# A decoder layer on one core: the first h chunk by hand within the first weight piece, and a few steps later in the order

## The chip, the core and the metric

The kernel runs on one core of a Trainium2 chip. Five engines work side by side, each through its own queue in program order: TensorE (PE, matrix products; PEld is its weight load), VectorE (DVE), ScalarE (ACT), GpSimd (POOL) and SyncE (SP), which here issues nearly all DMAs. The metric is the device time of one execution in microseconds, as the median of several runs. A profile is one further execution, recorded instruction by instruction.

## The reference, cut to what matters

One layer of a hybrid decoder, 256 tokens of width 2048, in float32:

```python
shift, scale, gate = jnp.split(jax.nn.silu(c) @ w_ada + b_ada, 3, axis=-1)
h = rms_norm(x, norm_pre_w) * (1.0 + scale[:, None]) + shift[:, None]
proj = h @ w_in
...
y_a = o_a.reshape(b, s, GDN_V_WIDTH).astype(x.dtype) @ w_proj_gdn
...
h_b = jax.nn.sigmoid(ml_o) * h_b * jax.nn.silu(ml_z)
y_b = h_b.astype(x.dtype) @ w_proj_mlstm
merged = jax.nn.sigmoid(gate_a) * y_a + jax.nn.sigmoid(gate_b) * y_b
out = merged @ w_out
return x + gate[:, None] * rms_norm(out, norm_post_w)
```

Between proj and y_a stands a gated delta rule (GDN), between proj and y_b an mLSTM, both in chunks. What matters here: no product with w_in can begin before h is there, and h needs the statistics of x and, for each of 16 chunks of 128 channels, a shift and a scale, which are sums over a row of w_ada.

## The kernel before, in words

**Products.** Every product of weights is made of three in float32r: operands are split into a high part (a cast on ScalarE, L169) and a low part (a subtraction on VectorE or POOL, L170), and mm3 (L223) adds hi x hi, hi x lo and lo x hi into one PSUM tile. split_w (L174 on) decides by a running share which low parts POOL makes; VectorE makes the others.

**The stream.** Weights come as units of up to one megabyte through three buffers (load_w, tile raw). A unit is used in pieces of 1024 columns. Stream.run fixes the order by hand: it prepares pieces (casts and low parts) as long as no more than `ahead` of them are pending, then issues the products of one piece, then calls side.step(). The work beside the products, attention and gates, stands in generators; each gets one turn per step, and `yield` means one step later. Each engine runs what it is given in the order of issue. Units of w_ada (tile ar, three buffers) stand in the same stream without products: VectorE multiplies one with silu(c) along the row and sums it (L353). w_ada units 2k and 2k + 1 give the shift and the scale of chunk k.

**The start groups.** Fourteen groups of 512 columns of w_in are accumulated in seven blocks over the chunks of h (BLOCKS), so that products can begin when chunk 0 alone is known: the first block takes groups 0 to 5 over chunk 0, two groups to a unit, the second groups 6 to 13 over chunks 0 and 1, and so on. Sums between the blocks are kept in SBUF (part): a copy on ScalarE in the first two blocks (L411, some on VectorE, L413), an addition on VectorE later (L409). In the last block the finished group gets Sigmoid or Silu at once (L418), and is stored to DRAM (L420) or multiplied with its neighbour and stored (L422, L423).

**The start itself.** SyncE issues c, the two halves of c_row, x, an identity, two small tables, and then the stream's loads. c_row gets Silu and is spread over all partitions by eight TensorE instructions on one row (L280). The sums of squares of x go to ScalarE and VectorE (L291, L292), the power to POOL. Then ScalarE scales x by its row statistics, two chunks at a time (x_scale, L300), TensorE turns them (x_turn, L306) and ScalarE copies them back (L308): chunks 0 to 7 are scaled, and 0 to 3 turned, ahead of the stream; the others behind the w_ada units. h_chunk (L327 to L331) makes shift, scale, hf, and its two parts h_hi and h_lo.

**Later places.** gates (L455 on) computes decay and gate rows beside the last block and ends in transposes (L507, L508). mlstm_out (L992) turns the finished mLSTM output, gated by gated_by (L1023). merge (L1181 to L1190) adds the two branches and turns the sum for the last product.

Of the kernel before, what the change touches and what calls it, by code (L numbers as in the profile page):

```python
# [117 lines left out]
def hybrid_layer_kernel(  # L118
# [50 lines left out]
        A.copy(hi, src)  # L169
        (eng or V).tensor_tensor(lo, src, hi.bitcast(F32), op=ALU.subtract)  # L170

    share = [-3072.0, START_SHARE]

    def split_w(src, hi, lo):  # L174

# [50 lines left out]
    bp = x0 = y0 = None  # L226


    ct = const("ct", c_t, [P, KC])
    sil = cp.tile([P, KC], F32, name="sil")  # L230
    A.activation(sil, ct, AF.Silu)
# [37 lines left out]
    crow = [part[4 + i].rearrange("p b c -> p (b c)")[0:1] for i in range(2)]  # L269
    for i in range(2):  # L270
        SP.dma_start(crow[i], c_row[:, i * 1024:(i + 1) * 1024])
    for b in range(2):
        SP.dma_start(xs[:, b], x[b * P:(b + 1) * P])
    SP.dma_start(ident, consts[:, 0:128])
    bat = const("bat", b_ada_t, [P, 32])
    npre = const("npre", npre_t, [P, KC])
    for i in range(2):
        A.activation(crow[i], crow[i], AF.Silu)
    for q in range(4):
        T.matmul(csil[:, q * 512:(q + 1) * 512], one_row, crow[q // 2][:, (q % 2) * 512:(q % 2 + 1) * 512],  # L280
                 start=True, stop=True)
    late_c = {}

    def late_consts():
        SP.dma_start(con[:, 128:512], consts[:, 128:512])
        late_c.update(gcv=const("gcv", gconv, [P, 256]), mcv=const("mcv", mconv, [P, 64]),
                      abb=const("abb", ab_bias, [P, 1]), alog=const("alog", a_log, [32, 1]),
                      gnw=const("gnw", gnorm, [P, 1]), mnw=const("mnw", mnorm_t, [P, KC]))

    for b in range(2):  # L290
        A.activation(part[2].rearrange("p b c -> p (b c)"), xs[:, b, 0:1024], AF.Square, accum_out=ss[:, b, 0:1])  # L291
        V.scalar_tensor_tensor(part[3].rearrange("p b c -> p (b c)"), xs[:, b, 1024:D], 1.0, xs[:, b, 1024:D],  # L292
                               op0=ALU.mult, op1=ALU.mult, accum_out=ss[:, b, 1:2])
    V.tensor_reduce(rs, ss, axis=AX.X, op=ALU.add)
    V.tensor_scalar(rs, rs, 1.0 / D, EPS, op0=ALU.mult, op1=ALU.add)
    pow_(rs, rs, mhalf[:, 0:2])

    def x_scale(k):
        for b in range(2):
            A.activation(xs[:, b, k * P:(k + 2) * P], xs[:, b, k * P:(k + 2) * P], AF.Copy, scale=rs[:, b:b + 1])  # L300

    def x_turn(k):
        ps = jtile("xps")
        for b in range(2):
            for kk in range(2):
                T.transpose(ps[:, (b * 2 + kk) * P:(b * 2 + kk + 1) * P], xs[:, b, (k + kk) * P:(k + kk + 1) * P],  # L306
                            ident)
        A.copy(xs[:, :, k * P:(k + 2) * P], ps.rearrange("p (b c) -> p b c", b=2))  # L308
# [9 lines left out]
    V.scalar_tensor_tensor(bnp, bat[:, KC:2 * KC], 1.0, npre, op0=ALU.add, op1=ALU.mult)  # L318

    def load_ada(src):  # L320
        raw = sp.tile([P, 2048], F32, name="ar", tag="ar", bufs=ADA_BUFS)
        SP.dma_start(raw, src)
        return raw

    def h_chunk(k):

        A.activation(sh[:, k:k + 1], ad[:, k:k + 1], AF.Identity, bias=bat[:, k:k + 1])  # L327
        A.activation(s1[:, k:k + 1], ad[:, KC + k:KC + k + 1], AF.Identity, bias=bnp[:, k:k + 1],
                     scale=npre[:, k:k + 1])
        hf = sp.tile([P, S], F32, name="hf", tag="hf", bufs=2)  # L330
        A.activation(hf.rearrange("p (b t) -> p b t", b=2), xs[:, :, k * P:(k + 1) * P], AF.Identity, bias=sh[:, k:k + 1], scale=s1[:, k:k + 1])  # L331
        split(hf, h_hi[:, k], h_lo[:, k], V if k < 2 else G)

    stream = Stream(load_w, side, 2)
    NG, NE = len(START), 6
# [11 lines left out]
    def ada_units():  # L347

        adders = []
        for k in range(KC):  # L350
            for pt in range(2):
                def prep(h, raw, k=k, pt=pt):
                    V.scalar_tensor_tensor(raw, raw, 1.0, csil, op0=ALU.mult, op1=ALU.mult,  # L353
                                           accum_out=ad[:, pt * KC + k:pt * KC + k + 1])
                    j = 2 * (2 * k + pt) - 4
                    if 4 <= j < 16:
                        x_turn(j)
                        if j < 12:
                            x_scale(j + 4)
                    h_chunks(k - 1)  # L360
                    if pt == 1:
                        due.append(k)
                        if k == 0:
                            h_chunks(0)
                        elif k == KC - 1:
# [27 lines left out]
    def add_start_groups(bi):  # L393
# [12 lines left out]
        def after(g, ps):  # L406
            for b in range(2):
                if k0:
                    V.tensor_tensor(part[g][:, b], ps[b], part[g][:, b], op=ALU.add)  # L409
                elif bi or g < 4 or b == 0:  # L410
                    A.copy(part[g][:, b], ps[b])  # L411
                else:
                    V.tensor_copy(part[g][:, b], ps[b])  # L413
            if bi == len(BLOCKS) - 2 and g == 3:
                late_consts()
            if lastb:
                pt = part[g].rearrange("p b c -> p (b c)")
                A.activation(pt, pt, AF.Silu if g in (9, 11, 13) else AF.Sigmoid)  # L418
                if g < 8:
                    SP.dma_start(gate_dr[g], part[g])  # L420
                elif g % 2:
                    V.tensor_tensor(part[g], part[g], part[g - 1], op=ALU.mult)  # L422
                    SP.dma_start(gate_dr[8 + (g - 8) // 2], part[g])  # L423
                if g == NG - 1:
                    branches_open()

        adders = []
# [22 lines left out]
    def gates(ps):  # L450
# [50 lines left out]
        A.activation(g2[64:72], bm[64:72], AF.Exp, scale=-1.0)  # L501
# [22 lines left out]
        stream.add(w_ab, prep_w, use, after=lambda: side.add(gates(st_["ps"])))  # L524

    ada = ada_units()
    ia = 0
    for bi, (groups, k0, nk, first, last) in enumerate(BLOCKS):
        if bi == len(BLOCKS) - 1:
            add_ab()  # L530
        fs = add_start_groups(bi)
        for j, f in enumerate(fs):
            ahead = first + (last - first) * j / len(fs)
            while ia < len(ada) and ia < ahead:
                ada[ia]()
                ia += 1
            f()

# [217 lines left out]
    def gdn_stage2(zg, res, zr):  # L756
# [116 lines left out]
        for g, z, h, c in heads:  # L873
# [127 lines left out]
    def mlstm(m):  # L1001
# [29 lines left out]
        def gated_by(sg, first):  # L1031
            while "hn" not in r or not (first or "gated" in r):
                yield
            for b in range(2):
                gate(b, sg[:, b], first)
            r["gated"] = True
            yield
            if not first:
                yield from mlstm_out(m, r)

        def gated():
# [128 lines left out]
    def merge(hf, yb):  # L1170
# [213 lines left out]
```

## Time and profile before

| | before |
|---|---|
| median of 3 runs | 1620.76 us (1618.08 to 1620.88) |
| the profiled execution | 1616.79 us |
| its span | 1615.0 us |
| TensorE, products, share of the span | 98% |
| VectorE, ScalarE, POOL | 71%, 58%, 15% |
| DMA | 372.37 MB, 231 GB/s in the mean |

A row of the order of time gives the start, the duration, engine, line, operation and tiles, how many instructions were merged into the row, and in brackets the idle time ahead with what ended it. A row of waits gives who waited, for whom, the microseconds in total, the times and the longest. Products overlap in the pipeline, so a product's duration is longer than the distance between the starts of two.

### The profile page before, as it was taken

The page shows a single profiled execution, that of the slowest core. Times are in us where ns is not written, and L with a number is a line of the kernel's source. Part 1 is how long each engine was busy: PE and PEld are TensorE (multiplying, and loading weights), DVE is VectorE, ACT ScalarE, POOL GpSimd, SP SyncE. Part 2 cuts the span into 40 slices and gives each one's busy share as a digit, 9 for nine tenths or more (in the row PEclk, how much of TensorE's full clock was granted, in tenths as well). Part 3 has the DMA queues.
Part 4 walks back from the last instruction along what each step waited for, and adds up shares of the span by engine and source line. Part 5 has one row for each costly group of instructions (what it writes and reads, how often), then busy time and mean ns, then how long its engine had stood idle before and what let it go on. Part 6 is the DMA issues. An engine that isn't in the chain of part 4 may idle for free.

```text
span 1615.0 us, 25449 instructions
## 1 busy us (share of the span) xinstructions
PE 1585.7 (98%) x9844; PEld 1388.1 (86%) x9844; DVE 1148.3 (71%) x1798; ACT 936.4 (58%) x1497; POOL 235.2 (15%) x191
## 2 busy tenths in 40 slices
PE   7999999899999999999999999999999999999998
PEld 4888888689999999999999999889988788888886
DVE  6685555675689878887888888776778556756654
ACT  7744445664666575757666666664665544444443
POOL 1787761000000000000000000000010000100100
PEclk9999999999999999999999999999999999999999
DMA  9898775665555546454646464557778668767573
GB/s 375 342 408 334 263 286 191 236 244 204 181 182 191 183 170 193 171 191 158 205 159 197 157 196 169 184 211 246 281 291 315 222 247 293 280 233 250 196 275 115
DMA packets 96261, 372.37 MB, mean 231 GB/s; under 512 B 26262, under 2 KB 46214, under 8 KB 58252
## 3 DMA queue, kind: packets, MB, share of 16 engines
q1 hardware_dynamic: 96140, 370.75, 64.5%
q8 instruction: 77, 1.26, 0.3%
q14 instruction: 44, 0.36, 0.1%
HBM read 354.40 MB, written 16.31 MB: 230 GB/s over the span
## 4 chain that ended last, share of the span: by engine, by line
PE 88%; DVE 3%; ACT 3%; issue 2%; DMA 2%; POOL 1%; SPq 0%; DVEq 0%; POOLq 0%; ACTq 0%
PE pn L223 31%; PE pt L223 29%; PE py L223 16%; PE pw L223 5%; ACT whi L169 2%; DVE wlo L170 1%; DMA raw<-in_dram 1%; DVE part L409 1%; PE psa L223 1%; DMA ar<-in_dram 1%; PE mz L808 1%; PE mq L799 1%; PE po L848 0%; PE pa L820 0%; PE pc L838 0%
## 5 line engine op out<-in xcount | busy, mean ns | idle before, releaser
L170 DVE TENSOR_TENSOR wlo<-raw,whi 128x1024 fp32r<-128x1024 f32 x454 | 560.6, 1245 | 266.6 <-ACT whi L169 265.4
L169 ACT CAST whi<-raw 128x1024 fp32r<-128x1024 f32 (+1 forms) x517 | 532.1, 1046 | 314.3 <-PE pn L223 148.8
L223 PE MATMUL pt<-h_hi,whi 128*128 128x256 f32 x1280 | 368.8, 288 | 0.0
L223 PE MATMUL pt<-h_hi,wlo 128*128 128x256 f32 x1280 | 363.0, 284 | 0.0
L223 PE MATMUL pt<-h_lo,whi 128*128 128x256 f32 x1280 | 362.8, 283 | 0.0
L223 PE MATMUL pn<-whi,h_hi 128*128 128x512 f32 x896 | 354.2, 395 | 7.9 <-ACT whi L169 5.8
L223 PE MATMUL pn<-wlo,h_hi 128*128 128x512 f32 x896 | 351.1, 392 | 3.3 <-DVE wlo L170 2.5
L223 PE MATMUL pn<-whi,h_lo 128*128 128x512 f32 x896 | 349.9, 390 | 0.0
L223 PEld LDWEIGHTS pt<-h_hi,whi 128*128 128x128 f32 x1280 | 246.0, 192 | 1.4
L223 PEld LDWEIGHTS pt<-h_lo,whi 128*128 128x128 f32 x1280 | 246.2, 192 | 0.3
L223 PEld LDWEIGHTS pt<-h_hi,wlo 128*128 128x128 f32 x1280 | 246.0, 192 | 0.0
L223 PEld LDWEIGHTS pn<-whi,h_hi 128*128 128x128 f32 x896 | 168.7, 188 | 45.7 <-ACT whi L169 6.2
L223 PEld LDWEIGHTS pn<-wlo,h_hi 128*128 128x128 f32 x896 | 168.7, 188 | 41.6 <-DVE wlo L170 7.4
L223 PEld LDWEIGHTS pn<-whi,h_lo 128*128 128x128 f32 x896 | 168.5, 188 | 35.3
L170 POOL TENSOR_TENSOR wlo<-raw,whi 128x1024 fp32r<-128x1024 f32 (+1 forms) x63 | 146.1, 2327 | 67.2 <-ACT whi L169 65.0
L223 PE MATMUL py<-whi,yhi 128*128 128x512 f32 x384 | 150.6, 392 | 0.0
L223 PE MATMUL py<-whi,ylo 128*128 128x512 f32 x384 | 149.6, 390 | 0.0
L223 PE MATMUL py<-wlo,yhi 128*128 128x512 f32 x384 | 149.5, 389 | 0.0
L409 DVE TENSOR_TENSOR part<-pn,part 128x512 f32<-128x512 f32 x112 | 73.5, 685 | 52.4 <-PE pn L223 52.4
L169 ACT CAST yhi<-ya 128x512 fp32r<-128x512 f32 x48 | 29.9, 622 | 131.7 <-PE py L223 129.0
L170 DVE TENSOR_TENSOR ylo<-ya,yhi 128x512 fp32r<-128x512 f32 x48 | 33.2, 691 | 91.3 <-ACT yhi L169 89.5
L585 DVE SCALAR_TENSOR_TENSOR qs<-pt,gcv,qs 128x255 f32<-128x255 f32 (+2 forms) x192 | 92.1, 480 | 4.6
(244 smaller groups left out, 1785.2 us busy)
## 6 DMA issues: line engine op xcount, KB each, us to landing
raw<-in_dram SPq DMA_DIRECT2D x259, 1024.0 KB
ar<-in_dram SPq DMA_DIRECT2D x32, 1024.0 KB
raw<-in_dram SPq DMA_DIRECT2D x16, 512.0 KB
ya<-o_dr SPq DMA_DIRECT2D x32, 256.0 KB
gate_dr<-part SPq DMA_DIRECT2D x11, 512.0 KB
gb<-rows SPq DMA_DIRECT2D x20, 256.0 KB
raw<-in_dram SPq DMA_DIRECT2D x6, 768.0 KB
ug<-ud SPq DMA_DIRECT2D x32, 128.0 KB
```

What stands on the lines that cost most here:

```text
L169: A.copy(hi, src)
L170: (eng or V).tensor_tensor(lo, src, hi.bitcast(F32), op=ALU.subtract)
L223: T.matmul(ps, l, r, start=start and i == 0, stop=stop and i == 2, skip_group_check=True)
L409: V.tensor_tensor(part[g][:, b], ps[b], part[g][:, b], op=ALU.add)
L585: V.scalar_tensor_tensor(dst[:, n, sh:], src[:, 0:S - sh], taps(n, 3 - sh), dst[:, n, sh:], op0=ALU.mult, op1=ALU.add)
L799: T.matmul(psp[64:128, m * 64:(m + 1) * 64], um(m)[0:64, 64:128], y0[:, m], start=True, stop=True)
L808: T.matmul(psz[0:64, m * 64:(m + 1) * 64], p2[64:128, m], x0[64:128, m, 64:128], start=True, stop=True)
```

## The change

1. The DMA of c and its Silu move from the start to late_consts, behind other late loads; the Silu is two steps behind.
2. c_row goes as one DMA into an ar buffer, issued by ScalarE's queue. w_ada unit 0 (the shift of chunk 0) is loaded ahead of x, unit 1 (its scale) in two halves behind x and the tables. The two no longer stand in the stream, which begins with a weight unit.
3. Chunk 0 is made by hand inside the preparation of the first weight piece (first_chunk): five products of zeros; sums of squares, three quarters on ScalarE; statistics on POOL; the sums of the two w_ada units on VectorE, the second by halves; the cast of the weights; scaling and turning of chunks 0 and 1; one more product of zeros; the low part of the weights; hf straight from PSUM, h_hi, h_lo; the copy of chunk 1.
4. Scaling of chunks 2 to 7 and the turn of 2 and 3 move from the start to behind groups 1, 3 and 5 of the first block.
5. The values of a finished group (Sigmoid or Silu, store) become a side generator of rank 0 that begins one step later; the product of two neighbours comes one further step later.
6. One step more: before the gates' transposes, before the transposes of the last GDN group (`2 + zg // 7`), before mlstm_out of the first mLSTM group, before the merge's transposes.
7. POOL's share of low parts starts from -2048 instead of -3072, as the first piece is no longer counted.

The core of the diff:

```diff
-    share = [-3072.0, START_SHARE]
+    share = [-2048.0, START_SHARE]
+    begin = []
...
+        if begin:
+            begin.pop()(raw[:, 0:n], hi, lo)
+            return hi, lo
...
+    crow = ada_tile()[0:1]
+    A.dma_start(crow, c_row)
+    ar0, ar1 = load_ada(w_ada[0]), ada_tile()
     for b in range(2):
         SP.dma_start(xs[:, b], x[b * P:(b + 1) * P])
...
+        SP.dma_start(ar1[:, i * 1024:(i + 1) * 1024], w_ada[1][:, i * 1024:(i + 1) * 1024])
...
+    def keep_busy(n):
+
+        for _ in range(n):
+            T.matmul(zps, zero[:, 0:P], zero, start=True, stop=True)
...
-    for k in range(0, 8, 2):
-        x_scale(k)
-        if k in (2, 4):
-            x_turn(k - 2)
...
+    def first_chunk(src, hi, lo):
+
+
+        keep_busy(5)
...
+        G.tensor_tensor(rs, ss[:, :, 0], ss[:, :, 1], op=ALU.add)
+        G.tensor_scalar(rs, rs, 1.0 / D, EPS, op0=ALU.mult, op1=ALU.add)
+        pow_(rs, rs, mhalf[:, 0:2])
+        ada_sum(ar0, slice(0, D), ad[:, 0:1])
+        V.scalar_tensor_tensor(bnp, bat[:, KC:2 * KC], 1.0, npre, op0=ALU.add, op1=ALU.mult)
+        for i in range(2):
+            ada_sum(ar1, half[i], adh[:, i:i + 1])
+        V.tensor_tensor(ad[:, KC:KC + 1], adh[:, 0:1], adh[:, 1:2], op=ALU.add)
+        V.scalar_tensor_tensor(s1[:, 0:1], ad[:, KC:KC + 1], npre[:, 0:1], bnp[:, 0:1], op0=ALU.mult, op1=ALU.add)
+        A.activation(sh[:, 0:1], ad[:, 0:1], AF.Identity, bias=bat[:, 0:1])
+        A.copy(hi, src)
+        x_scale(0)
+        xps = x_turn(0)
+        keep_busy(1)
+        V.tensor_tensor(lo, src, hi.bitcast(F32), op=ALU.subtract)
+        hf = sp.tile([P, S], F32, name="hf", tag="hf", bufs=2)
+        A.activation(hf.rearrange("p (b t) -> p b t", b=2), xps[:, :, 0], AF.Identity, bias=sh[:, 0:1],
+                     scale=s1[:, 0:1])
+        split(hf, h_hi[:, 0], h_lo[:, 0], V)
+        A.copy(xs[:, :, P:2 * P], xps[:, :, 1])
+    begin.append(first_chunk)
...
-                pt = part[g].rearrange("p b c -> p (b c)")
-                A.activation(pt, pt, AF.Silu if g in (9, 11, 13) else AF.Sigmoid)
...
+                side.add(gate_values(g), 0)
...
+        def gate_values(g):
+
+            yield
+            pt = part[g].rearrange("p b c -> p (b c)")
+            A.activation(pt, pt, AF.Silu if g in (9, 11, 13) else AF.Sigmoid)
...
+                    if bi == 0 and gg in (1, 3, 5):
+                        x_scale(gg + 1)
+                        if gg == 1:
+                            x_turn(2)
...
-        yield from wait(2)
+        yield from wait(3)
         tp = gtile("tp")
...
-        yield from wait(2)
+        yield from wait(2 + zg // 7)
         yield from free(4)
...
             if not first:
+                yield
                 yield from mlstm_out(m, r)
...
-        yield
+        yield from wait(2)
         for k2 in range(hf * 4, hf * 4 + 4):
```

More of the change, by code (lines that the diff above doesn't have):

```diff
@@ L268, in hybrid_layer_kernel, with ada_tile, load_ada @@
     csil = pcs.enter_context(tc.tile_pool(name="pcs", bufs=1, space=PSUM)).tile([P, D], F32, name="csil")
-    crow = [part[4 + i].rearrange("p b c -> p (b c)")[0:1] for i in range(2)]
-    for i in range(2):
-        SP.dma_start(crow[i], c_row[:, i * 1024:(i + 1) * 1024])
+    def ada_tile():
+        return sp.tile([P, 2048], F32, name="ar", tag="ar", bufs=ADA_BUFS)
+    def load_ada(src):
+        raw = ada_tile()
+        SP.dma_start(raw, src)
+        return raw
+    crow = ada_tile()[0:1]
+    A.dma_start(crow, c_row)
+    ar0, ar1 = load_ada(w_ada[0]), ada_tile()
     for b in range(2):
@@ new lines, in x_turn, with ada_sum @@
+        return ps.rearrange("p (b k t) -> p b k t", b=2, k=2)
+    bnp = sp.tile([P, KC], F32, name="bnp")
+    adh = sp.tile([P, 2], F32, name="adh")
+    def ada_sum(raw, cols, out):
+        V.scalar_tensor_tensor(raw[:, cols], raw[:, cols], 1.0, csil[:, cols], op0=ALU.mult, op1=ALU.mult,
+                               accum_out=out)
+    def first_chunk(src, hi, lo):
+        keep_busy(5)
+        half = [slice(i * 1024, (i + 1) * 1024) for i in range(2)]
+        for b in range(2):
+            for i in range(2):
+                if b == 0 and i == 1:
+                    V.scalar_tensor_tensor(part[3].rearrange("p b c -> p (b c)"), xs[:, b, half[i]], 1.0,
+                                           xs[:, b, half[i]], op0=ALU.mult, op1=ALU.mult, accum_out=ss[:, b, i:i + 1])
+                else:
+                    A.activation(part[2].rearrange("p b c -> p (b c)"), xs[:, b, half[i]], AF.Square,
+                                 accum_out=ss[:, b, i:i + 1])
+        G.tensor_tensor(rs, ss[:, :, 0], ss[:, :, 1], op=ALU.add)
[3 more added lines that the diff above has]
+        V.scalar_tensor_tensor(bnp, bat[:, KC:2 * KC], 1.0, npre, op0=ALU.add, op1=ALU.mult)
+        for i in range(2):
+            ada_sum(ar1, half[i], adh[:, i:i + 1])
[12 more added lines that the diff above has]
+        A.copy(xs[:, :, P:2 * P], xps[:, :, 1])
@@ L349, in ada_units @@
         adders = []
-        for k in range(KC):
+        for k in range(1, KC):
             for pt in range(2):
@@ L533, in hybrid_layer_kernel @@
             ahead = first + (last - first) * j / len(fs)
-            while ia < len(ada) and ia < ahead:
-                ada[ia]()
+            while ia - 2 < len(ada) and ia < ahead:
+                ada[ia - 2]()
                 ia += 1
@@ L1038, in gated_by @@
             if not first:
+                yield
                 yield from mlstm_out(m, r)
```

50 lines of the change are left out of this document (22 added, 28 removed).

## Prediction

> **What bounds the kernel now.** I read the page first, then the waits of TensorE, then each engine's order of time in the first 36 us, then the other places where TensorE waits.
>
> ```profile
> span 1615.0 us, 25449 instructions
> PE 1585.7 (98%) x9844; PEld 1388.1 (86%) x9844; DVE 1148.3 (71%) x1798; ACT 936.4 (58%) x1497; POOL 235.2 (15%) x191
> ```
>
> ```profile
> PE pn L223 <- ACT whi L169: 5.8, 1, 5.8
> PE csil L280 <- ACT part L278: 3.9, 1, 3.9
> PE pn L223 <- DVE wlo L170: 2.5, 6, 0.6
> PE mpt L992 <- DVE hn L1023: 1.8, 2, 1.5
> PE pn L223 <- DVE part L409: 1.6, 3, 0.7
> PE tp L508 <- ACT work L501: 1.1, 1, 1.1
> ```
>
> TensorE is busy 98% of the span. Its real products stay as they are, so a change can win only where TensorE stands or runs slowly: ahead of its first real product, in the last block of the start groups, at the mLSTM output, at the merge. For the first place, SyncE's first and fourth issue, then VectorE, ScalarE and TensorE:
>
> ```profile
> 0.74 0.39 SPq L157 DMA_DIRECT2D ct<-in_dram  x1
> ```
>
> ```profile
> 1.82 0.83 SPq L273 DMA_DIRECT2D xs<-in_dram  x2
> ```
>
> ```profile
> 15.14 2.29 DVE L353 SCALAR_TENSOR_TENSOR ar<-ar,csil 128x2048 f32<-128x2048 f32 x1
> ```
>
> ```profile
> 17.90 0.60 ACT L331 ACTIVATE hf<-xs,sh,s 128x256 f32<-128x256 f32 x1
> 18.53 0.40 ACT L169 CAST h_hi<-hf 128x256 fp32r<-128x256 f32 x1
> 18.84 1.99 ACT L169 CAST whi<-raw 128x1024 fp32r<-128x1024 f32 x2
> 21.68 1.04 ACT L169 CAST whi<-raw 128x1024 fp32r<-128x1024 f32 x1 [0.86 <-DMA raw<-in_dram]
> ```
>
> ```profile
> 3.92 7.19 PE L280 MATMUL csil<-part,one_row 1*128 1x512 f32 x8 [3.92 <-ACT part L278]
> 12.20 1.97 PE L306 MATMUL xps<-con,xs 128*128 128x128 f32 x8 [1.09 <-ACT xs L300]
> 19.93 0.79 PE L223 MATMUL pn<-whi,h_hi 128*128 128x512 f32 x1 [5.76 <-ACT whi L169]
> ```
>
> ```profile
> 24.80 0.39 PE L223 MATMUL pn<-whi,h_lo 128*128 128x512 f32 x1
> 25.03 0.40 PE L223 MATMUL pn<-whi,h_hi 128*128 128x512 f32 x1
> ```
>
> The second w_ada unit is summed from 15.14; hf, h_hi and the first weight cast then stand in a row on ScalarE, and the first real product starts at 19.93. The product at 25.03 is the thirteenth, the first of the second weight unit. One starts 0.23 us after another (24.80, 25.03), so twelve should take 2.7 us; they took 5.1. The stretches just behind decide most of my forecast:
>
> ```profile
> 24.00:34.00 10.00, 10.00 (x46) 7.78 (x45) 8.09 (x10) 8.97 (x17) 0.96 (x1) 1.00 1.01 403
> 34.00:49.00 15.00, 13.81 (x66) 10.68 (x65) 7.04 (x8) 14.94 (x28) 11.77 (x6) 1.00 1.02 418
> ```
>
> The columns behind the length are the busy times of TensorE, its weight loads, VectorE, ScalarE and POOL, then clock, DMA share and GB/s. ScalarE has 8.97 of 10 us and then 14.94 of 15; TensorE loses 1.2 us in the second. In the ramp ScalarE is the bound.
>
> **The start.** SyncE no longer issues c and c_row ahead of x; the shift unit goes first, so the first megabyte is issued at 0.74 instead of 1.82. The DMA share is 1.01 and 1.02, so all that follows keeps its place in a full queue and lands 1.08 us earlier. The first piece of weights is half a megabyte behind the second w_ada unit (in by 15.1); at 403 GB/s that is 1.3 us: 16.4 before, 15.3 after. The third unit's weights come at 21.68 - 1.08 = 20.6.
>
> Now by hand on ScalarE: the cast of the first weights from 15.3 to 16.4, two scalings of x to 17.3 (0.5 each, below), four transposes on TensorE to 17.7 (1.97 us for eight, partly under the scalings), hf 0.60, h_hi 0.40. The first real product starts at 18.8, 1.1 us earlier. The last half of the scale unit lands at 15.1 - 1.1 = 14.0; its sum is half of 2.29, behind the other sums on VectorE at 16.3. The row statistics go to POOL; three operations at no more than the 0.70 of this row end by 15.1, ahead of the scalings:
>
> ```profile
> 10.90 0.70 POOL L219 TENSOR_TENSOR rsx<-rsx,mhalf 128x2 f32<-128x2 f32 x1 [10.46 <-DVE bnp L318]
> ```
>
> The weights' low part is ready by 17.9, so the twelve products run without the waits of before, to 21.5.
>
> The products of zeros are not in the trace. The nearest rows are fp32 products of 512 columns: csil, 7.19 / 4 = 1.80 us each, and gps, 4.1 / 4 = 1.03:
>
> ```profile
> L1091 PE MATMUL gps<-gacc,ones 128*1 128x512 f32 x8 | 4.1, 591 | 0.0
> ```
>
> Five take 5.1 to 9.0 us. From csil's end at 10.7 (c_row has a queue of its own, I take 0.4 earlier) they end between 15.8 and 19.7. I take 17.2, the first half at the slow price: just in time for the transposes. The sixth lies behind the transposes and is hidden until 18.8. Their worth is that real products start at full clock. csil was slow for all of its 7.19 us, so products on one row did not open the clock; real products had opened it by 24.80. [...] If zeros behave as csil did, the time is that of the second rival.
>
> Then what is moved behind the first products. Before, the scalings of chunks 2 to 7 and the turn of chunks 2 and 3 lay in ScalarE's free time ahead of 17.9. Now they are issued behind groups 1, 3 and 5. From the groups of ScalarE, 20 to 49 us:
>
> ```profile
> L411 ACT COPY part<-pn 128x512 f32<-128x512 f32 x20 | 11.3, 591 | 1.5 <-PE pn L223 0.7
> L169 ACT CAST whi<-raw 128x1024 fp32r<-128x1024 f32 x10 | 10.4, 1051 | 0.9 <-DMA raw<-in_dram 0.9
> L300 ACT ACTIVATE xs<-xs,rsx 128x256 f32<-128x256 f32 x6 | 2.8, 527 | 0.0
> ```
>
> A pair of scalings is 2.8 / 3 = 0.9 us, a copy out of PSUM 0.5 where it follows another. ScalarE gets three pairs and two copies, 2.7 + 0.9 = 3.6 us, and loses one cast, 1.0, to its free time. Step by step: the third unit's cast is issued ahead of the first copies and waits for its weights to 20.6, so it ends at 21.6. Four copies end at 23.5, the pair for chunks 2 and 3 at 24.4. TensorE has the transposes of these chunks next in its own queue, ahead of the second unit: it stands from 21.5, and the second unit starts at about 24.7, against 25.03. The early start is spent there. The pairs for chunks 4 to 7 then lie ahead of the next two casts; the second of these, at 31.91, moves to 33.2 (1.8 for the pairs, less 0.3 and some free time). Its low part is POOL's, and a product waits for that:
>
> ```profile
> 31.91 1.05 ACT L169 CAST whi<-raw 128x1024 fp32r<-128x1024 f32 x1
> ```
>
> ```profile
> 33.04 2.38 POOL L170 TENSOR_TENSOR wlo<-raw,whi 128x1024 fp32r<-128x1024 f32 x1 [21.44 <-ACT whi L169]
> ```
>
> ```profile
> 35.48 0.50 PE L223 MATMUL pn<-wlo,h_hi 128*128 128x512 f32 x1 [0.61 <-POOL wlo L170]
> ```
>
> It starts at 36.7 instead of 35.48. From there ScalarE is full to 49, so nothing is made up: **start, +1.2 us**. Bounds: -3.4 if the transposes do not hold TensorE (1.1, and 5.1 - 2.7 = 2.4 less 0.1), +4 with a slow clock. I take +1.2, as it follows ScalarE's own rows.
>
> **The last block of the start groups.** A group's Sigmoid or Silu is issued one step later (twelve products, 2.7 us), with its store to DRAM. Waits of ScalarE and of TensorE from 262 to 346:
>
> ```profile
> ACT part L418 <- DVE part L409: 25.0, 12, 4.0
> ```
>
> ```profile
> PE pn L223 <- DVE wlo L170: 2.0, 5, 0.6
> PE tp L508 <- ACT work L501: 1.1, 1, 1.1
> PE pn L223 <- DVE part L409: 1.0, 2, 0.7
> ```
>
> ScalarE stood 25.0 us for the groups' sums, the next casts queued behind; TensorE paid 2.0 + 1.0 for it, and 1.1 for the gates' transposes, which get a step more too. A step later the sums are done. Each of the eight stalls also makes its product 0.1 longer (0.50 at 35.48, 0.40 at 25.03): 4.1 + 0.8 = **-4.9**; bounds -3 and -6.
>
> **mLSTM output and merge.** A step more before the transposes takes away the 1.8 us of waiting and 0.2 of restart. Behind that gap the clock fell:
>
> ```profile
> 1088.80:1092.10 3.30, 1.61 (x12) 1.45 (x13) 3.30 (x6) 2.53 (x6) 0.00 (x0) 1.00 0.53 223
> 1092.20:1095.50 3.30, 3.30 (x17) 3.21 (x16) 3.30 (x4) 0.95 (x2) 0.00 (x0) 0.50 0.65 174
> ```
>
> Half the clock for some 3.4 us costs 1.7. With products in the gap it should stay: 2.0 + 1.7 = **-3.7**; bounds -1 (an execution without the slow stretch, part of the wait kept) and -4. The merge has a step more as well:
>
> ```profile
> PE mtp L1190 <- POOL mg L1181: 0.6, 1, 0.6
> ```
>
> That is **-0.7** with the restart. The step added for the last GDN group, the later load and Silu of c: nothing, hidden by TensorE's products, as no wait of TensorE names them; without that cover a few tenths.
>
> **Sum.** 1.2 - 4.9 - 3.7 - 0.7 = -8.1. The profiled execution took 1616.8 us (span 1615.0 and 1.8 around it), so 1608.7. The median of the three runs is 1620.8, 4.0 above it, and I carry that over: 1612.7.
>
> **Rivals.** *ScalarE keeps up*, and the transposes do not hold TensorE: the free time between its copies speaks for it, the order of the queues against it. Start -3.4, total -12.7: 1608.1. *Zeros do not open the clock*: five end at 19.7, transposes at 20.6, and the sixth holds the first product to 22.4; twelve products take 2.7 + 1.7, and the two copies, the pair and the transposes hold the second unit to 28.6, so start +4 and total -5.3: 1615.5. For it is csil's row, against it that csil used one row of the array. *The waits only move*: the later Sigmoid meets the next group's casts and TensorE still loses 4.9: 1617.6. *Slower*: SyncE's queue in that last block, where each store waits for its Sigmoid with the next weight load behind it:
>
> ```profile
> SPq L420 <- ACT part L418: 31.2, 8, 5.0
> ```
>
> With three buffers a load is read two units (10.8 us) after its buffer comes free, and a megabyte takes 2.6 at 403 GB/s, so a hold decides only from about 8 us on; one step is 2.7. At 9 us each of the 8 waits of this row costs 1 and the 4.9 are not won: 1.2 - 4.4 + 8 = +4.8, 1625.6.
>
> **How the numbers follow.** Forecast 0.50, ScalarE keeps up 0.17, slow zeros 0.14, waits only move 0.12, slower 0.07. Runs of before spread over 2.8 us, so 0.2% (3.2 us) is about what can be told from no change. Faster by that: 0.48 + 0.17 + 0.11 + 0.04 = 0.80; same 0.13; slower 0.07. The range runs from the first rival, with the last block at its better bound, to the third: 1606.5 to 1618.
>
> **What would show it.** Right: the first real product near 18.8 and starts 0.23 apart at once; TensorE standing at the transposes of chunks 2 and 3 until about 24.4; POOL's first low part ending near 36.7; ScalarE no longer waiting for the sums at L409; full clock at 1092. Wrong: a first product at 21 or later; the second unit at 21.6; weights landing late from 262 to 346.

## The result and the profile after

| | before | after |
|---|---|---|
| median of 5 runs | 1620.69 us (1618.08 to 1620.88) | 1609.68 us (1607.69 to 1611.40) |
| profiled execution, its span | 1616.79, 1615.0 | 1611.40, 1609.5 |
| a second profiled execution, its span | 1614.21, 1612.1 | 1608.21, 1606.3 |

The ratio is 0.9934 (95% interval 0.9921 to 0.9948). That is faster by 11.0 us; forecast was 1612.7, in a range that holds the result. The page of the kernel after, first lines:

```profile
span 1609.5 us, 25475 instructions
PE 1588.7 (99%) x9856; PEld 1390.1 (86%) x9856; DVE 1147.4 (71%) x1797; ACT 937.7 (58%) x1498; POOL 239.1 (15%) x195
```

Twelve products more (six of zeros, each recorded as two), and TensorE still stands for less of the span, in part because the zeros count as busy (their rows last 8.5 us, 10.89 to 18.39 and 19.20 to 20.22). The waits of TensorE over the whole span, of after:

```profile
PE csil L294 <- ACT ar L292: 3.8, 1, 3.8
PE xps L328 <- ACT xs L321: 2.0, 1, 2.0
PE pn L227 <- DVE part L459: 1.7, 1, 1.7
PE pn L227 <- POOL wlo L170: 1.6, 2, 1.4
PE pnum L1023 <- issue: 1.3, 1, 1.3
PE pt L948 <- DVE on L939: 0.9, 1, 0.9
```

The wait for csil stays. The 5.8 us ahead of the first product are filled with zeros and not won, as the first real product starts no earlier in this profile (below). The 2.5 for low parts are down to 0.3, and the 1.8 for hn and the 1.1 for the gates are gone. New or longer are the wait at the transposes of chunks 2 and 3 (L328), that for POOL's low part, and a wait for VectorE's addition (L459) that the prediction did not have.

**Where the time went.** A place in the order of work can be followed from kernel to kernel by the first start of a tile. The tile view gives it as the first of the two times ("first and last start us"). First before, then after:

```profile
L223 PE MATMUL pab<-h_hi,whi x16: 278/283/383, 256.9 to 262.5; 128*128 128x256 f32 x16
...
L223 PE MATMUL psa<-qh x16: 396/397/498, 401.7 to 1001.0; 128*128 128x512 f32 x16
```

```profile
L227 PE MATMUL pab<-h_hi,whi x16: 278/283/383, 262.0 to 267.6; 128*128 128x256 f32 x16
...
L227 PE MATMUL psa<-qh x16: 396/396/498, 398.8 to 998.1; 128*128 128x512 f32 x16
```

pab is the last adapter call, ahead of the last block of start groups; psa is the first score product of the GDN behind it. Up to pab the changed kernel is 5.1 us late, and from pab to psa it takes 136.8 us instead of 144.8. The same view of both profiles of both kernels, with pnum (mLSTM) and py and pw (the last projections):

| first start of | before | after | before, second | after, second |
|---|---|---|---|---|
| first real product | 19.9 | 20.5 | 19.8 | 19.5 |
| first product of the second weight unit | 25.0 | 26.2 | 25.2 | 25.2 |
| pab | 256.9 | 262.0 | 257.5 | 259.4 |
| psa | 401.7 | 398.8 | 402.2 | 396.3 |
| pnum | 1066.4 | 1063.5 | 1066.9 | 1061.0 |
| py | 1248.2 | 1243.4 | 1245.3 | 1240.3 |
| pw | 1518.2 | 1512.7 | 1515.3 | 1509.5 |

So, by stretches, first pair and second pair: start +5.1 and +1.9; last block -8.0 and -7.8; mLSTM (pnum to py) -1.9 and +0.9; projections with the merge (py to pw) -0.7 and -0.8; the rest nothing.

**The start.** ScalarE of after from the first weights on, then TensorE:

```profile
17.01 1.04 ACT L365 CAST whi<-raw 128x1024 fp32r<-128x1024 f32 x1 [3.39 <-DMA raw<-in_dram]
...
22.11 1.06 ACT L169 CAST whi<-raw 128x1024 fp32r<-128x1024 f32 x1 [0.45 <-DMA raw<-in_dram]
23.07 2.04 ACT L461 COPY part<-pn 128x512 f32<-128x512 f32 x4
24.98 0.94 ACT L321 ACTIVATE xs<-xs,rsx 128x256 f32<-128x256 f32 x2
```

```profile
20.50 0.50 PE L227 MATMUL pn<-whi,h_hi 128*128 128x512 f32 x1 [0.28 <-ACT h_hi L169]
20.84 0.40 PE L227 MATMUL pn<-wlo,h_hi 128*128 128x512 f32 x1
21.07 0.40 PE L227 MATMUL pn<-whi,h_lo 128*128 128x512 f32 x1
...
25.57 0.83 PE L328 MATMUL xps<-con,xs 128*128 128x128 f32 x4 [2.04 <-ACT xs L321]
26.16 0.48 PE L227 MATMUL pn<-whi,h_hi 128*128 128x512 f32 x1
```

The order on ScalarE is that of the prediction: cast, four copies, the pair of scalings, and TensorE stands at the transposes behind it for 2.04 us. All of it lies later, because the first weights were cast at 17.01, not 15.3; 3.39 us of waiting for their DMA stand ahead. Starts are 0.23 apart from the second product on; without the zeros they are 0.43 apart (run No zeros, below). The stretches around that gap (columns as in the prediction, clock the last but two):

```profile
23.70:27.10 3.40, 1.53 (x8) 1.21 (x9) 3.40 (x4) 2.80 (x6) 0.00 (x0) 1.00 1.04 433
27.10:30.50 3.40, 3.40 (x10) 2.64 (x9) 1.37 (x2) 1.76 (x3) 0.00 (x0) 0.50 1.03 419
```

TensorE was busy for 1.53 of 3.40 us, and then had half the clock for 3.4 us, 1.7 us lost. In the second profile of after the clock stayed:

```profile
27.00:30.40 3.40, 3.40 (x17) 2.82 (x16) 0.51 (x2) 3.21 (x6) 0.00 (x0) 1.00 1.02 418
```

There TensorE starts the same work like this:

```profile
19.54 0.50 PE L227 MATMUL pn<-whi,h_hi 128*128 128x512 f32 x1 [0.28 <-ACT h_hi L169]
...
24.62 0.83 PE L328 MATMUL xps<-con,xs 128*128 128x128 f32 x4 [2.05 <-ACT xs L321]
25.21 0.48 PE L227 MATMUL pn<-whi,h_hi 128*128 128x512 f32 x1
...
37.33 0.50 PE L227 MATMUL pn<-wlo,h_hi 128*128 128x512 f32 x1 [1.39 <-POOL wlo L170]
```

The gap is the same, 2.05 us, and the clock did not fall. As the second profiles have no such stretch, "the second pair" is the cleaner comparison for the start from here on.

**The wait at 88 us.** VectorE of after, first profile:

```profile
83.18 2.17 DVE L170 TENSOR_TENSOR wlo<-raw,whi 128x1024 fp32r<-128x1024 f32 x1 [0.44 <-ACT whi L169]
85.27 2.27 DVE L405 SCALAR_TENSOR_TENSOR ar<-ar,csil 128x2048 f32<-128x2048 f32 x1
...
87.47 2.28 DVE L405 SCALAR_TENSOR_TENSOR ar<-ar,csil 128x2048 f32<-128x2048 f32 x1
...
89.68 1.88 DVE L459 TENSOR_TENSOR part<-pn,part 128x512 f32<-128x512 f32 x3
```

A low part and two w_ada sums, 6.5 us together, lie ahead of the addition that empties the PSUM tile TensorE waits for. By the starts of products it costs 1.9: the start at 90.51 lies 2.09 behind the one ahead, where 0.23 is usual. In before the same place cost 0.7 (a start 0.92 behind the one ahead, at 85.38), and 1.9 and 1.1 in the second profiles of after and before.

**The last block.** ScalarE's waits from 262 to 346, of after; before it was 25.0 us in 12 waits for the same line (25.0 as well with the start alone, 7.8 with the last block alone):

```profile
ACT part L475 <- DVE part L459: 6.7, 7, 1.8
```

TensorE's waits there are all gone but one, which before had as well:

```profile
PE pab L227 <- POOL h_lo L170: 0.4, 1, 0.4
```

### The profile page after: what moved, and what is told of

Read it like the earlier page. It is cut to its first block, busy times and chain, and to the rows that moved or that the text cites. A ratio compares the mean times of both kernels' runs of the same rounds, so it can differ in the third digit from the quotient of the medians.

```text
span 1609.5 us, 25475 instructions
## 1 busy us (share of the span) xinstructions
PE 1588.7 (99%) x9856; PEld 1390.1 (86%) x9856; DVE 1147.4 (71%) x1797; ACT 937.7 (58%) x1498; POOL 239.1 (15%) x195
## 4 chain that ended last, share of the span: by engine, by line
PE 93%; DMA 3%; issue 2%; DVE 1%; ACT 1%; POOL 0%; DVEq 0%; SPq 0%; POOLq 0%; ACTq 0%
PE pn L227 35%; PE pt L227 28%; PE py L227 16%; PE pw L227 5%; DMA raw<-in_dram 2%; PE psa L227 1%; DMA ar<-in_dram 1%; PE mz L868 0%; PE mq L859 0%; PE pa L880 0%; PE po L908 0%; PE pc L898 0%; PE po L909 0%; PE pb L888 0%; PE po L906 0%
## 5 line engine op out<-in xcount | busy, mean ns | idle before, releaser
L169 ACT CAST whi<-raw 128x1024 fp32r<-128x1024 f32 x516 | 531.7, 1046 | 326.8 <-PE pn L227 149.7
L459 DVE TENSOR_TENSOR part<-pn,part 128x512 f32<-128x512 f32 x112 | 73.6, 685 | 52.3 <-PE pn L227 52.3
## 6 DMA issues: line engine op xcount, KB each, us to landing
ya<-o_dr SPq DMA_DIRECT2D x32, 256.0 KB
gb<-rows SPq DMA_DIRECT2D x20, 256.0 KB
```

## The experiments

Each ran beside the kernel before on the same chip; differences are of medians, and the interval is that of the ratio to before. The medians of before differ from place to place by up to 2.3 us (1618.4 to 1620.7), so a run set beside the median of after is also given against its own before, where after has -11.0.

**The start alone.** Of the change only points 1 to 4 and 7; the gate values at once and no added steps, as before.

```diff
-                side.add(gate_values(g), 0)
+                pt = part[g].rearrange("p b c -> p (b c)")
+                A.activation(pt, pt, AF.Silu if g in (9, 11, 13) else AF.Sigmoid)
...
-        yield from wait(3)
+        yield from wait(2)
```

> The change of the start alone (first chunk by hand, scalings moved, c later), with the gate values at once and without the added steps. Theory A, that the start loses: in the profiles the first product of the gate unit (pab) starts at 262.0 us after the change and at 256.9 before, so this kernel should show about 262 there and take 4 to 6 us more than before, about 1625. Theory B, that the profiled execution was a poor one and the start on its own wins 1 to 3 us in the median: 1618 to 1620, pab ahead of 257. Theory C, my sum on record, +1.2: 1622, pab near 258.

Measured: 1621.64 against 1618.72, +2.9 us (ratio 1.0010 to 1.0028, 11 runs against 15). TensorE again stands at the transposes (1.94 us) and pab starts at 259.3. Taken alone the new start makes the kernel slower, by more than the sum on record (theory C, +1.2) and less than theory A said (4 to 6).

**The rest alone.** The kernel before with points 5 and 6.

```diff
+                side.add(gate_values(g), 0)
...
-        yield from wait(2)
+        yield from wait(2 + zg // 7)
...
-        yield
+        yield from wait(2)
```

> Gate values one step later and the added steps (gates, last GDN group, mLSTM output, merge), with the start as before. Theory A: the whole gain is here and more, the start gave some back: 5 us below the changed kernel, about 1605; pab at 257, and no wait of ScalarE for the sums at the gate values. Theory B: the start wins too, so this one is slower than the changed kernel, 1611 to 1613. By my sum on record, 9.3 below before: 1611.4.

Measured: 1606.9 against 1618.72, -11.8 us (0.9913 to 0.9938). All of the gain lies here. The two halves add up to -8.9 us; the -11.0 of both together goes beyond that by 2.1, which lies within its interval (-8.4 to -12.8).

**The last block alone.** The kernel before with the later gate values and wait(3) ahead of the gates' transposes.

```diff
+                side.add(gate_values(g), 0)
...
-        yield from wait(2)
+        yield from wait(3)
         tp = gtile("tp")
```

> The kernel before with the later gate values and the one step more ahead of the gates' transposes, nothing else of the change. Theory, that a stall of TensorE costs some 0.25 us more than the wait that is listed for it (the distances of the starts say so), so that eleven stalls of 4.5 us listed are worth 7 to 8: the time falls by 7 to 8 to about 1611.5, and the first score product comes 136.9 us behind the first product of the last adapter call instead of 144.8. Rival, the prediction's price of 4.9 from the list of waits: 1614.

Measured: 1609.22 against 1618.38, -9.2 us (0.9931 to 0.9959, that is -6.6 to -11.2). The tile view gives 136.8 us from pab to psa:

```profile
L223 PE MATMUL pab<-h_hi,whi x16: 277/283/384, 258.2 to 263.8; 128*128 128x256 f32 x16
...
L223 PE MATMUL psa<-qh x16: 396/396/498, 395.0 to 994.7; 128*128 128x512 f32 x16
```

The price of 4.9 falls; 8.0 holds. Most of the change is thus the values of a group moved behind one `yield`, with one step more ahead of the gates' transposes; the two were not run apart, and by the starts of before the stall at those transposes (L508, at 308) is 1.3 of the 8.0.

**The late steps undone.** After, without the added step ahead of the last GDN group's transposes, of mlstm_out and of the merge's transposes.

```diff
-        yield from wait(2 + zg // 7)
+        yield from wait(2)
...
-                yield
                 yield from mlstm_out(m, r)
...
-        yield from wait(2)
+        yield
```

> The changed kernel without the three added steps of the later stages (last GDN group, mLSTM output, merge); the gates' extra step and the later gate values stay. Theory, the sum on record: the wait at the mLSTM output, the half clock behind it and the wait at the merge come back, +4.4, 1614. Rival: as other stretches of the same stage lose more in the profile after than before (1.45 us at 1193, 1.04 at 1083), the waits only move and the steps are worth 1 to 2 us: 1611 to 1612.

Measured: 1613.72 against before's 1619.51 (0.9955 to 0.9978), 4.0 above the median of after (-5.8 against its own before). Its waits and its clock:

```profile
PE mpt L1052 <- DVE hn L1083: 1.8, 2, 1.5
```

```profile
1084.80:1088.10 3.30, 1.39 (x36) 0.96 (x36) 3.22 (x8) 3.02 (x6) 0.00 (x0) 1.00 0.83 303
1088.20:1091.60 3.40, 3.40 (x18) 3.40 (x18) 3.40 (x4) 1.77 (x3) 0.00 (x0) 0.50 0.42 58
```

Wait and half clock are back. The half clock is not bound to come, though: in the second profile of before TensorE waits for hn as well (1.3 us), and the stretch that had 0.50 in the first reads

```profile
1092.20:1095.50 3.30, 3.30 (x71) 3.13 (x71) 2.12 (x2) 1.97 (x6) 0.00 (x0) 1.00 0.83 253
```

Nor does the added step keep it away for certain: the profile of the kernel called Both (below), which has that step, shows in the same place

```profile
1080.30:1083.70 3.40, 3.40 (x19) 3.40 (x18) 3.40 (x7) 2.31 (x5) 0.00 (x0) 0.50 0.45 188
```

Over all profiles half clock stands behind the mLSTM output in three of the five executions without the step (before once, last block alone, late steps undone) and in one of the nine with it.

**No zeros.** After, with neither of the two groups of products of zeros.

```diff
-        keep_busy(5)
...
-        keep_busy(1)
```

> The changed kernel without the products of zeros. Theory: the zeros opened the clock (granted 1.00 from 16.8 in the profile after); without them the twelve products of the first unit run at half clock for some 3.4 us and start at about the same place, so the second unit's wait for the scalings is reached later but ends at the same place, and most of the loss is hidden in it: 0 to 1.5 us slower than the changed kernel, 1610 to 1611. Rival 1: as the forecast had it, full price 1.7 us and the later scalings with it, 1612. Rival 2: the zeros hold TensorE up (transposes at 18.5 behind them) and without them it is faster, 1609 or less.

Measured: 1610.62 against 1619.51 (0.9933 to 0.9960, that is -6.5 to -10.8); the interval overlaps that of after. The median is 0.9 above that of after (2.1 with each against its own before). TensorE:

```profile
19.81 0.79 PE L227 MATMUL pn<-whi,h_hi 128*128 128x512 f32 x1 [1.14 <-ACT h_hi L169]
20.40 0.63 PE L227 MATMUL pn<-wlo,h_hi 128*128 128x512 f32 x1
...
26.38 0.84 PE L320 MATMUL xps<-con,xs 128*128 128x128 f32 x4 [1.08 <-ACT xs L313]
26.97 0.48 PE L227 MATMUL pn<-whi,h_hi 128*128 128x512 f32 x1
```

Without zeros the twelve products take twice as long: 0.43 from start to start, against 0.23 with them. 0.43 is also the distance in after where 0.50 of the clock was granted (starts at 27.24 and 27.67). The clock column itself reads 1.00 in before and after from the start of the span to 27 us, also where before's products start 0.43 apart (22.21 and 22.64), so half clock at the start is read from the distances alone. But 1.0 of what is lost comes back at the transposes, where TensorE stands 1.08 instead of 2.05. Beside the second profile of after, 1.8 us of loss are left at the second unit (26.97 against 25.21) and at pab (261.2 against 259.4): the wait for ScalarE hides less than half of what the slow starts cost (2.4 for the twelve products).

**The turn later.** After, with the turn of chunks 2 and 3 two groups later.

```diff
-                        x_scale(gg + 1)
-                        if gg == 1:
+                        if gg == 3:
                             x_turn(2)
+                        x_scale(gg + 1)
```

> The changed kernel with the turn of chunks 2 and 3 two groups later (behind group 3, ahead of the scaling of chunks 4 and 5), so that TensorE does not wait for scalings it has just been given. Theory A1, that this wait (2.0 us at 23.5) and the half clock behind it (27.1 to 30.5) are most of the loss: pab 3 to 4 us earlier than in the changed kernel, about 258, and 1606. Theory A2, that ScalarE's load is the bound: the wait goes, the low parts of the fifth piece are late all the same, at most 1 us won: pab near 261, 1609.

Measured: 1606.27 against 1618.72, -12.4 us (0.9911 to 0.9938). The wait at the transposes is gone and the second unit starts 2.7 us earlier than in the second profile of after:

```profile
22.52 0.50 PE L227 MATMUL pn<-whi,h_hi 128*128 128x512 f32 x1 [0.19 <-ACT part L461]
```

Its pab starts at 260.5 all the same, in an execution whose wait for VectorE's addition had grown to 2.8 us with half the clock behind it (0.50 from 87.3 to 90.7). The time is that of theory A1, pab that of A2; this run by itself does not decide between them.

**Scaling first.** After, with scaling and turn of chunks 0 to 3 ahead of the first cast of weights, where ScalarE waits for the DMA.

```diff
-        keep_busy(5)
+        keep_busy(3)
...
-        A.copy(hi, src)
         x_scale(0)
         xps = x_turn(0)
-        keep_busy(1)
+        x_scale(2)
+        x_turn(2)
+        keep_busy(3)
+        A.copy(hi, src)
...
-                    if bi == 0 and gg in (1, 3, 5):
+                    if bi == 0 and gg in (3, 5):
                         x_scale(gg + 1)
-                        if gg == 1:
-                            x_turn(2)
```

> The changed kernel with the scaling and the turn of chunks 0 to 3 ahead of the cast of the first weights, in the 3.4 us in which ScalarE waits for them, the zeros in two parts of three, and the two other scalings behind groups 3 and 5. Theory A2, ScalarE's load is the bound: 1.4 us at the first product (19.1 instead of 20.5), no wait at 23.5, 1.5 us less of scalings and copies in the ramp: pab 4 to 6 us earlier than in the changed kernel, 256 to 258, and 1604 to 1606. Rival, the DMA bounds the ramp whatever ScalarE does: the early start is given back at the next weights, pab stays at 261 to 262 and the time at 1609.

Measured: 1606.53 against 1618.72, -12.2 us (0.9913 to 0.9938), pab at 257.1. This is 3.1 below the median of after (1.2 with each against its own before). At pab it is 4.9 earlier than the first profile of after and 2.3 earlier than the second. The first product starts at 19.58, no earlier than in the second profile of after and not at the 19.1 of the theory; the second unit starts at 22.84 instead of 25.21, and that is the gain. So the pair of scalings and the turn of chunks 2 and 3 held the second unit; the other two pairs are still behind groups 3 and 5. The rival, that the DMA bounds the ramp, is out.

**Another phase of POOL's share.** In the changed kernel the first piece is no longer counted. Started from -2252.8 (-3072 plus one piece's 0.8 x 1024), the pieces go to POOL in the same turn as before; from -2048 they don't.

```diff
-    share = [-2048.0, START_SHARE]
+    share = [-2252.8, START_SHARE]
```

> The changed kernel with the share of low parts starting from -2252.8, so that the same pieces as before go to POOL and VectorE (with -2048 the sixth piece goes to POOL and not to VectorE, and all later turns of VectorE fall on another piece). Theory: the 1.9 us wait of TensorE for VectorE's addition at 88.4, behind a low part and two w_ada sums, comes from the shifted turns: it shrinks to the 0.7 of before and the time to 1608 or 1608.5. Rival: that wait comes with the later start of everything, and nothing changes: 1609.7 (within 0.7).

Measured: 1607.77 against 1619.51 (0.9920 to 0.9943), 1.9 below the median of after (0.7 with each against its own before); the intervals overlap. The wait for the addition shrinks from 1.70 to

```profile
86.89 0.47 PE L227 MATMUL pn<-whi,h_hi 128*128 128x512 f32 x1 [0.33 <-DVE part L459]
```

**Both.** Scaling first, with this share.

> Scalings and turn of chunks 0 to 3 ahead of the first cast (as in e5_scale_first, 1606.5) and the share from -2252.8. Theory: the two add up, pab near 255.5 and 1605. Rival: 1606.5 as without it.

Measured: 1604.71 against 1619.51 (0.9900 to 0.9926, 4 runs), the lowest median of all, and pab at 256.0, ahead of before. What is left in the start is POOL's low part:

```profile
23.17 0.50 PE L227 MATMUL pn<-whi,h_hi 128*128 128x512 f32 x1 [0.51 <-ACT part L463]
...
35.30 0.50 PE L227 MATMUL pn<-wlo,h_hi 128*128 128x512 f32 x1 [1.39 <-POOL wlo L170]
```

**That low part on VectorE**, on top of both.

```diff
-            split(src, hi, lo, G)
+            split(src, hi, lo, G if len(share) > 2 else V)
+            share.append(0)
```

> On top of the fastest order so far (scaling and turn ahead of the casts, shorter share at the start), VectorE makes the low part of the fifth piece instead of GpSimd. Theory, that the product waits at 33 us for GpSimd's slow low part (2.38 us there against 1.23 on VectorE): that wait of 1.6 us goes, the time falls by about 1 to 1603.5 to 1604. Rival, that VectorE's added 1.2 us only moves the wait to the next part that it owes: same time, 1604.7, and a wait for VectorE between 33 and 45 us.

Measured: 1605.65 against 1618.8 (0.9907 to 0.9934): no gain over the run before it. The 1.39 us are gone, and smaller waits for VectorE and ScalarE behind them give it all back: from the second unit to pab the delays between the starts of products add up to 4.1 us in both, and pab starts at 256.0 in both. The rival held:

```profile
34.04 0.50 PE L228 MATMUL pn<-wlo,h_hi 128*128 128x512 f32 x1 [0.19 <-DVE wlo L170]
...
37.38 0.50 PE L228 MATMUL pn<-wlo,h_hi 128*128 128x512 f32 x1 [0.33 <-DVE wlo L170]
```

**Each kernel profiled again**, unchanged.

> A second profile of the kernel before. [...]

> A second profile of the changed kernel. Clock by chance: no half clock at 27.1 to 30.5 us or one of another place, and the first product of the last adapter call earlier than 262 us by up to 1.7. Clock by program: both as in the first profile.

Measured: 1614.21 and 1608.21. Neither stretch of half clock came again (1.00 from 27.00 to 30.40 in after and from 1092.20 to 1095.50 in before), and pab of after lies 2.6 earlier (1.7 of it the clock, 0.9 the earlier landing of the first weights, whose cast starts at 16.05). The waits of the last block stand as they were in before. So the waits belong to the program; whether the clock fell behind them changed from the first execution to the second.

## Why the prediction was right, and where it was off

**Direction and cause: right.** Faster, because TensorE's stalls in the last block of start groups go; the start gives nothing, because ScalarE's scalings hold the transposes of chunks 2 and 3. The runs with the start alone (+2.9), the rest alone (-11.8) and the last block alone (-9.2) show this. That the time came within 3.0 of the forecast is partly luck: of the four terms only the merge had its size, and the errors cancel in part. (The lower end of the range is also 0.5 below its own working: 1608.1 with the last block at its better bound is 1607.0.)

**The start: predicted +1.2; +1.9 and +5.1 in the two pairs of profiles, +2.9 in its own run.** Over all profiles pab starts at 256.9 to 258.8 with the old start (before twice, rest alone, last block alone; 257.8 in the mean) and at 259.3 to 262.0 with the new one unaltered (after twice, start alone, late steps undone; 260.6): +2.8. The mechanism came step by step. Worked out were 18.8 for the first product, 24.4 for the end of the stand, 24.7 for the second unit and 36.7 for the product behind POOL's low part; the second profile of after has 19.5, 24.6, 25.2 and 37.3. Three things were mis-sized or missing:
- "In by 15.3" for the first weights. The cast starts at 16.05 and 17.01. The sum took 403 GB/s throughout; here are the two microseconds from 10 to 12 of after and then of the second profile, where the queue is full and moves 228 and 248:

```profile
10.00:12.00 2.00, 2.00 (x4) 0.59 (x3) 1.00 (x1) 1.20 (x3) 0.00 (x0) 1.00 0.99 228
```

```profile
10.00:12.00 2.00, 2.00 (x4) 0.69 (x3) 1.09 (x1) 1.20 (x3) 0.00 (x0) 1.00 1.01 248
```

  At 403 that stretch would move 0.3 MB more, which is 0.8 us. Before has its dip at 8 to 10, at 356. All ten profiles with the new start have 223 to 260 from 10 to 12, so the dip belongs to the new order of loads. The small tables stand near that place in the queue; that they cause it was not tried. Both profiles of after have the dip, so it does not explain why the first cast starts 0.96 later in the first; that is open.
- The clock behind the stand at the transposes: 1.7 in the first profile, nothing in the second. The prediction had half clock behind a gap at the mLSTM output, but none behind the gap that it forecast itself.
- The share's start, which the prediction passed over. By the starts it costs 1.2 more at 88 us in the first pair (1.9 against 0.7) and 0.7 more in the second (1.9 against 1.1). The run with the old phase shows that the phase makes the wait, and Both against scaling first shows it again: the wait for the addition, listed with 1.7 without the old phase, is gone with it.

**The last block: predicted -4.9; -8.0 and -7.8.** The step that failed is the price of a stall: the listed wait and 0.1 of restart. The rows of before give more. Starts of two products stand 0.23 apart, yet at 297.61 and 298.71 they are 1.10 apart with 0.71 listed as idle, and the next start comes after 0.31:

```profile
297.61 0.39 PE L223 MATMUL pn<-whi,h_lo 128*128 128x512 f32 x1
298.71 0.47 PE L223 MATMUL pn<-whi,h_hi 128*128 128x512 f32 x1 [0.71 <-DVE part L409]
299.02 0.39 PE L223 MATMUL pn<-wlo,h_hi 128*128 128x512 f32 x1
```

A stall of 0.71 costs 0.87 + 0.08 = 0.95, that is 0.24 more than listed, since products overlap by 0.16 and the idle time counts only from the end of the last. Eight stalls make 4.1 + 1.9 = 6.0; the rest of the 8.0 are shorter delays that the list of waits doesn't hold, such as the starts 0.48 apart at 333.6 and 345.1. Added up over all products from pab to psa, starts stand 8.8 us further apart than the usual distance of their kind in before, and 1.0 in after. So the distances of starts, which lay in the trace of before, would have given the term.

**mLSTM output and merge: predicted -3.7 and -0.7.** The merge came as said. The mLSTM stretch (pnum to py) differs by -1.9 and +0.9, nearer to the upper bound of -1 that the prediction gave for an execution without the slow stretch. From the tile view of all profiles: five without the added step (before twice, start alone, last block alone, late steps undone) take 178.4 to 182.2, 180.5 in the mean; the nine with it 178.0 to 180.8, 179.3 in the mean. So some 1.2 us per execution, though the two ranges overlap almost whole. Most of that is the clock: with 1.7 taken off where a stretch of half clock stands (three of the five, one of the nine), the means are 179.5 and 179.1. The step that failed here is that the wait and its restart, 2.0, go: the wait for hn goes, but waits at pnum and pt stay or grow (1.3 and 0.9 in after), so that TensorE's listed waits in the stretch are 1.9 to 3.4 without the step and 1.1 to 3.3 with it. Against the medians the late steps are worth 2.7 (rest alone against last block alone) to 4.0 (undone; 5.2 with each against its own before); the intervals allow all of that. The runs point to the clock as well: the 40 with the late steps were granted 0.9982 in the mean, the 65 without them 0.9970, and 0.0012 of the span is 1.9 us.

**From the profile to the median: +4.0 carried over, and wrong.** In the profiles the kernel gains 5.4 and 6.0 us, in the medians 11.0. Both profiled executions of before (1616.8, 1614.2) lie below nearly all of its runs; those of after (1611.4, 1608.2) lie on both sides of its median. So the sum was too good by 2 to 3, the carry was too high by 3 to 6, and the forecast ended 3.0 above the result. Part of the difference between 5.4 to 6.0 and 11.0 may be the clock: each run comes with its mean granted clock, 0.001 of which is 1.6 us of this span, about one stretch of half clock. The 44 runs of before beside the experiments have 0.996 (10 runs, median 1619.6), 0.997 (14, 1619.3), 0.998 (19, 1618.0) and 0.999 (1, 1614.5); its two profiles have 0.998 and 0.999. The runs with the rest alone have 0.999 in four of five. Another part is the median of before beside this result: 1620.69, where the four groups of runs beside the experiments have 1618.4 to 1619.5. What each part is worth, and what the rest is, stays open, since no trace shows a run as slow as before's median.

**The rivals.** Zeros that leave the clock shut: out, by the rows of the run without them (0.43 from start to start, 0.23 with them). SyncE's queue held by the gate stores: out, the last block gained more than forecast and no product there waits for weights. Waits that only move: out there, though it is what happened to POOL's low part. ScalarE keeping up: not in this change. Scaling ahead of the cast takes the stand at the transposes away, but its pab (257.1) is level with before's (256.9 and 257.5) and not 3.4 ahead; that its 1606.5 lies near the 1608.1 worked out for this rival does not bear it out.

## What to carry to other kernels

Price a stall by the distances between starts, not by the list of waits, and price a step by the queue in which its instructions land: the Sigmoid, whose result nothing needs soon, held up the casts behind it on ScalarE, and one `yield` more there (with one for the gates' transposes) won 8 us; the scalings put ahead of the next copies lost 2 to 3. Work moved to make a start earlier belongs in the time in which its engine waits anyway, here ahead of the cast that waits for the DMA. And profile both kernels twice before comparing stages: here each had a stretch of half clock (0.50 for 3.4 us, 1.7 us lost) in its first profile, and none in that place in its second.

## What was not expected of the hardware

- Behind the products of zeros (128*128) the real products of after start 0.23 apart. Without the zeros, behind csil alone (1*128, 7.19 us) and 6.47 us without work ahead of the transposes, they start 0.43 apart. In the first profile of after the zeros' starts go from 0.85 to 0.43 apart at 16.9 (weight loads at 15.32, 16.18, 16.94 and 17.37). In the second this comes earlier: TensorE has five products from 14 to 16 us, where the first profile has three, though the program is the same.
- Half clock (0.50) stood behind stretches of 3.3 to 3.4 us in which TensorE was busy for 1.53 us (after, 23.7), 1.39 (late steps undone, 1084.8) and 1.61 (before, 1088.8), and even 2.47 (Both, 1077.0). In the second profile of after the clock read 1.00 (27.00 to 30.40) behind the same gap of 2.05 us, so the gap alone does not decide it; what does is not shown by these runs.
